# Latent attention layers: 96 query columns a head in three tiles instead of 128 in four, with the rotary swap moved to the keys

## The chip, the cores and the metric

One NeuronCore of a Trainium2 chip runs the whole program: a first block (a sparse and a gated linear mixer with a feed-forward part) and a second block of four attention layers on 512 tokens of width 1024, all in float32. The metric is the device time of one execution in microseconds.

## What is computed

Only layers 0 and 3 of the second block are touched. They are latent attention layers: queries come from a 384-wide latent `cq` through `w_q_up`, which gives each of 16 heads 96 columns, 64 plain and 32 that are rotated with the token's position.

```python
q = (_rmsnorm(cq, q_norm) @ w_q_up).reshape(B, S, MLA_HEADS, MLA_NOPE_DIM + MLA_ROPE_DIM)
q_rope = _apply_rope(q[..., MLA_NOPE_DIM:], cos[:, None, :], sin[:, None, :])
k_rope = _apply_rope(k_rope, cos, sin)
q_full = jnp.concatenate([q[..., :MLA_NOPE_DIM], q_rope], axis=-1)
scale = (MLA_NOPE_DIM + MLA_ROPE_DIM) ** -0.5
o = _dense_causal(q_full, k_full, v, scale).reshape(B, S, MLA_WIDTH)
# _apply_rope: x1, x2 are the halves of the 32 columns
jnp.concatenate([x1 * cos - x2 * sin, x2 * cos + x1 * sin], axis=-1)
```

## The kernel before

Every product is done three times (`mm3`, lines 269 to 277): each float32 operand is split by `split_into` into a high part (ScalarE, line 214) and a low part (VectorE, line 215), and the products high by high, low by high and high by low are added up in PSUM. Features stand on the partitions, the 512 tokens along the free dimension.

A latent layer works through four quads of four heads, and in each quad through two pairs (`pr`). Per quad it loads and splits `qw` (query weights), `kvw` (key and value weights) and the weights of two gate tiles, multiplies the values `vt`, and then, per pair, the keys of both heads into `k4h`, `k4l` and, per head, the queries. For the queries the weights are laid out with 128 columns: 64 plain, 32 rotary, and the same 32 again with halves swapped. So one product of 3 x 3 matmuls gives a `pj` tile of 128 rows, 64 of them x and swapped x. VectorE multiplies these 64 rows by a table of cosines and sines in place (line 1083), and `split_gain` makes `qh` (ScalarE, line 218) and `ql` (VectorE, line 219). The scores add the two rotary halves up by themselves, because the keys hold the same 32 rotated rows twice. `dense_head` then runs the softmax of the head block by block (scores `s` by line 273 ff., masked maximum line 324, exponent line 327, division line 331, transposes line 337), and `dense_values` multiplies by the values into `o` (line 350).

Instructions are ordered by the framework's scheduler at build time. Each engine runs its own list strictly in that order, so an instruction that waits holds up everything behind it. PSUM has three `pj` tiles, two `s`, two `t` and one `o`. `og` (8 tiles of 512 columns) holds the gated outputs of the layer, `vt` has two buffers, and the raw weight tile `wr` has three.

Of the kernel before, what the change touches and what calls it, by code (L numbers as in the profile page):

```python
# [18 lines left out]
S = 512  # L19
D = 1024  # L20
NB = 4
# [31 lines left out]
def shape_constants():  # L53
# [33 lines left out]
    sc = np.float32(96 ** -0.5)  # L87
    tab = np.empty((128, S), np.float32)
    for base in (0, 64):
        tab[base:base + 16] = tab[base + 16:base + 32] = cos.T * sc  # L90
        tab[base + 32:base + 48], tab[base + 48:base + 64] = -sin.T * sc, sin.T * sc
    out["mla_tab"] = tab
    kr = np.concatenate([cos, cos, -sin, sin], axis=1)
# [34 lines left out]
class Net:  # L128
# [857 lines left out]
    def mla(self, i, j, last):  # L986
        nc, a, tc = self.nc, self.a, self.tc
        w = a["mla_w_in_2"][j]
        with ExitStack() as c1:
            l1 = c1.enter_context(tc.tile_pool(name="l1", bufs=1))  # L990

            tab = self.load_const(l1, "mla_tab")
            scale = l1.tile([128, 2], F32, name="scale")
# [6 lines left out]
            with tc.tile_pool(name="pre", bufs=1) as pre:  # L1000
# [9 lines left out]
                for b in range(NB):  # L1010
                    ps = self.pj()
                    self.proj_tok(ps[:, 0:288], wk, self.act, b, cols=slice(0, 288))
                    self.low_rank(pre, cn[:, b, 384:640], ps, 256)
                    t = pre.tile([128, 64], F32, name="krt", bufs=2)
                    nc.vector.tensor_tensor(out=t[:, 0:32], in0=ps[:, 256:288], in1=kro[:, b, 0:32], op=ALU.mult)
                    nc.vector.tensor_tensor(out=t[:, 32:48], in0=ps[:, 272:288], in1=kro[:, b, 32:48], op=ALU.mult)
                    nc.vector.tensor_tensor(out=t[:, 48:64], in0=ps[:, 256:272], in1=kro[:, b, 48:64], op=ALU.mult)
                    for r0 in (0, 32, 64, 96):
                        nc.vector.tensor_tensor(out=kr[:, b, r0:r0 + 32], in0=t[:, 0:32], in1=t[:, 32:64], op=ALU.add)
                for c in range(6):  # L1020
# [17 lines left out]
            for quad in range(4):  # L1038

                qw = []  # L1040
                for pr in range(2):
                    v = self.wload(wqu, 0, 3, (quad * 384 + pr * 192, 192))
                    h, l = self.wtile(3, 256)
                    for u in range(2):
                        r, s0 = 64 - 64 * u, u * 96
                        pieces = ((0, 0, 96),) if u == 0 else ((192, 0, 64), (128, 64, 32))
                        for d, c, n in pieces + ((128 * u + r + 32, 80, 16), (128 * u + r + 48, 64, 16)):
                            self.split_into(h[:, :, d:d + n], l[:, :, d:d + n], v[:, :, s0 + c:s0 + c + n])
                    qw.append(Split([(0, 3, h, l)]))
# [21 lines left out]
                for pr in range(2):  # L1071
# [3 lines left out]
                    for hh in range(2):  # L1075
                        r = slice(64 * hh, 64 * hh + 64)
                        self.split_into(keys[hh][0][r], keys[hh][1][r], ps[r])
                    pt = []
                    for hh in range(2):
                        ps = self.pj()  # L1080
                        self.proj_feat(ps, qw[pr], cq, kc=3, cols=slice(hh * 128, hh * 128 + 128))
                        r = slice(64 - 64 * hh, 128 - 64 * hh)
                        nc.vector.tensor_tensor(out=ps[r], in0=ps[r], in1=tab[r], op=ALU.mult)
                        q = [l2.tile([128, S], F32R, name=n) for n in ("qh", "ql")]
                        self.split_gain(*q, ps, scale[:, hh:hh + 1])

                        def scores(ps, m, n):
                            (ah, al), (bh, bl) = ((t[:, m] for t in q), (t[:, n] for t in keys[hh]))
                            self.mm3(ps, [((ah, al), (bh, bl))])

                        pt.append(self.dense_head(P, scores))
# [253 lines left out]
```

## Time and profile before

| What | Value |
|---|---|
| time, median of 3 runs | 1871.92 us (1871.9 to 1871.92) |
| profiled execution | 1871.62 us, its span 1869.8 us |
| TensorE matmul busy (PE) | 1827.8 us, 98% of the span |
| VectorE busy (DVE) | 1149.3 us, 61% |
| ScalarE busy (ACT) | 873.6 us, 47% |
| granted TensorE clock | 0.999 of full speed |

The span runs from the first to the last instruction of the profiled execution; 1.8 us lie outside of it. A busy share is a mean over the whole span. Matmuls are pipelined, so the recorded length of one is longer than the distance to the next: the distance of the starts is what a matmul costs.

### The profile page before, as it was taken

To read this page: it belongs to the slowest core of one execution; us is meant where nothing else is said; L and a number is where in the kernel's file an instruction comes from. 1 tells how busy PE (TensorE), PEld (TensorE's weight loads), DVE (VectorE), ACT (ScalarE), POOL (GpSimd) and SP (SyncE) were. 2 spreads that over 40 slices of the span, in tenths; PEclk is the share of its full clock that TensorE was granted. 3 is DMA by queue.
4 is the path that set the end of the run, shared out by engine and by line. 5 is a ranking of instruction groups with operands and counts; after the bars stand their busy time and mean duration, and the time that the engine had idled before them with its cause. 6 is when DMAs were issued, how large, how long until landed. Compare 5 with 4: busy or idle time off the path is not lost.

```text
span 1869.8 us, 26625 instructions
## 1 busy us (share of the span) xinstructions
PE 1827.8 (98%) x9843; PEld 1489.1 (80%) x9843; DVE 1149.3 (61%) x2954; ACT 873.6 (47%) x1970; POOL 156.1 (8%) x213
## 2 busy tenths in 40 slices
PE   7999999999999999999999999999999999999997
PEld 6877787678888888889887788877888877988775
DVE  5564487854533244346878675576776666787866
ACT  4543336743322132235667434463566564366651
POOL 2211200000000000002000011241000000200001
PEclk9999999999999999999999999999999999999999
DMA  7222141042432253224221133221432322232111
GB/s 218 80 57 57 37 126 40 29 135 79 125 91 84 66 143 90 73 67 122 59 69 57 48 103 91 72 63 38 114 79 54 82 70 79 75 87 59 46 57 45
DMA packets 200781, 148.09 MB, mean 79 GB/s; under 512 B 8797, under 2 KB 178570, under 8 KB 200650
## 3 DMA queue, kind: packets, MB, share of 16 engines
q1 hardware_dynamic: 198858, 140.97, 26.2%
q0 software_dynamic: 1792, 5.42, 0.9%
q8 instruction: 77, 1.26, 0.3%
q14 instruction: 54, 0.44, 0.1%
HBM read 144.27 MB, written 2.10 MB: 78 GB/s over the span
## 4 chain that ended last, share of the span: by engine, by line
PE 91%; DVE 3%; ACT 2%; issue 2%; DMA 1%; POOL 0%; SPq 0%; POOLq 0%; DVEq 0%; ACTq 0%
PE pj L273 25%; PE pj L275 24%; PE pj L276 24%; PE o L350 4%; PE t L337 3%; PE s L311 1%; PE s L275 1%; PE s L273 1%; PE s L276 1%; PE t L372 1%; PE s L614 1%; PE s L312 1%; DVE wl L215 1%; ACT pt L205 1%; PE t L1198 1%
## 5 line engine op out<-in xcount | busy, mean ns | idle before, releaser
L214 ACT ACTIVATE wh<-wr 128x1024 fp32r<-128x1024 f32 (+9 forms) x390 | 280.4, 749 | 467.1 <-PE pj L275 279.8
L215 DVE TENSOR_TENSOR wl<-wr,wh 128x1024 fp32r<-128x1024 f32 (+9 forms) x390 | 321.7, 847 | 229.1 <-ACT wh L214 224.7
L273 PE MATMUL pj<-Ah,wh 128*128 128x512 f32 (+1 forms) x1120 | 435.4, 389 | 1.3 <-DVE k4l L215 0.8
L275 PE MATMUL pj<-Al,wh 128*128 128x512 f32 (+1 forms) x1120 | 434.1, 388 | 0.0
L276 PE MATMUL pj<-Ah,wl 128*128 128x512 f32 (+1 forms) x1120 | 433.5, 388 | 0.0
L273 PEld LDWEIGHTS pj<-Ah,wh 128*128 128x128 f32 x1120 | 210.8, 188 | 45.7 <-PE s L276 1.6
L276 PEld LDWEIGHTS pj<-Ah,wl 128*128 128x128 f32 x1120 | 210.8, 188 | 44.2 <-issue 1.5
L275 PEld LDWEIGHTS pj<-Al,wh 128*128 128x128 f32 x1120 | 210.8, 188 | 42.6 <-issue 0.8
L273 PE MATMUL pj<-wh,Ah 128*128 128x512 f32 (+5 forms) x640 | 217.6, 341 | 4.7 <-ACT Ah L214 4.6
L275 PE MATMUL pj<-wl,Ah 128*128 128x512 f32 (+5 forms) x640 | 215.7, 337 | 0.0
L276 PE MATMUL pj<-wh,Al 128*128 128x512 f32 (+5 forms) x640 | 213.3, 338 | 2.0 <-DVE Al L215 1.9
L327 ACT ACTIVATE sp<-sp,nm 128x128 f32<-128x128 f32 (+3 forms) x256 | 142.9, 559 | 75.5 <-DVE nm L326 73.4
L205 ACT ACTIVATE pt<-t 128x512 f32<-128x512 f32 (+3 forms) x288 | 115.2, 445 | 106.0 <-PE t L337 66.5
L324 DVE CUSTOM_DVE_ANT_0 sp<-s,c_causal 128x128 f32<-128x128 f32 (+3 forms) x256 | 121.0, 486 | 56.6 <-PE s L276 23.5
L273 PEld LDWEIGHTS pj<-wh,Ah 128*128 128x128 f32 x640 | 120.5, 188 | 19.5 <-ACT Ah L214 7.3
L276 PEld LDWEIGHTS pj<-wh,Al 128*128 128x128 f32 x640 | 120.2, 188 | 13.9 <-DVE Al L215 3.0
L275 PEld LDWEIGHTS pj<-wl,Ah 128*128 128x128 f32 x640 | 120.5, 188 | 10.8 <-issue 0.2
L337 PE MATMUL t<-ident,sp 128*128 128x128 f32 x640 | 109.0, 278 | 5.1 <-ACT pt L205 4.8
L337 PEld LDWEIGHTS t<-ident,sp 128*128 128x128 f32 x640 | 77.3, 140 | 30.8 <-ACT pt L205 12.7
L331 DVE TENSOR_SCALAR sp<-sp,rc 128x128 f32<-128x128 f32 (+3 forms) x256 | 96.7, 383 | 5.0
L276 PE MATMUL pj<-wh,hdl 128*128 128x512 f32 x176 | 68.3, 389 | 0.0
L275 PE MATMUL pj<-wl,hdh 128*128 128x512 f32 x176 | 68.3, 390 | 0.0
(417 smaller groups left out, 2822.5 us busy)
## 6 DMA issues: line engine op xcount, KB each, us to landing
wr<-in_w_in_dram SPq DMA_DIRECT2D x34, 512.0 KB, 3.9
wr<-in_fox_w_in_dram SPq DMA_DIRECT2D x30, 512.0 KB, 4.1
wr<-in_w_ffn_gate_dram SPq DMA_DIRECT2D x22, 512.0 KB, 3.8
wr<-in_w_ffn_up_dram SPq DMA_DIRECT2D x22, 512.0 KB, 3.8
wr<-in_w_ffn_down_dram SPq DMA_DIRECT2D x20, 512.0 KB, 3.7
wr<-in_swa_w_in_dram SPq DMA_DIRECT2D x20, 512.0 KB, 4.8
wr<-in_mla_w_in_dram SPq DMA_DIRECT2D x16, 512.0 KB, 4.3
wr<-in_mla_w_out_dram SPq DMA_DIRECT2D x16, 512.0 KB, 3.8
```

The costliest lines, as they stand in the source:

```text
L205: return self.nc.scalar.activation(out, in_, AF.Copy, scale=1.0 if scale is None else scale)
L214: self.nc.scalar.activation(h, src, AF.Copy)
L215: self.nc.vector.tensor_tensor(out=l, in0=src, in1=h.bitcast(F32), op=ALU.subtract)
L273: mm = self.nc.tensor.matmul(ps, lhsT=ah, rhs=bh, start=i == 0, stop=False)
L275: self.nc.tensor.matmul(ps, lhsT=ah, rhs=bl, start=False, stop=False)
L276: mm = self.nc.tensor.matmul(ps, lhsT=al, rhs=bh, start=False, stop=i == n - 1)
L311: self.nc.tensor.matmul(ps, lhsT=q, rhs=kh, start=True, stop=False)
L324: nc.vector.tensor_tensor_reduce(out=v, in0=ps, in1=self.causal[:, S - n:S], scale=1.0, scalar=LOWEST, op0=ALU.add, op1=ALU.max, accum_out ...
L327: nc.scalar.activation(v, v, AF.Exp, bias=nm[:, g], accum_out=sm[:, g])
L331: nc.vector.tensor_scalar(v, v, rc[:, g], None, ALU.mult)
L337: nc.tensor.transpose(ps[:, (b - j) * 128:(b - j + 1) * 128], sp[:, POFF[b] + j * 128:POFF[b] + j * 128 + 128], self.ident)
L350: mm = self.nc.tensor.matmul(po[64 * i:64 * i + 64, j * 128:S], lhsT=value(j, i), rhs=pt[:, TOFF[j]:TOFF[j] + (NB - j) * 128], start=first ...
```

## The change

The weights of a quad are laid out as three tiles of 128 columns with nothing twice: two tiles (`qw[0]`, 256 columns) each hold one head of the first pair whole and the rotary columns of one head of the second pair; one tile (`qw[1]`) holds the plain columns of both heads of the second pair. They are gathered by seven loads instead of two, and split by two operations an engine instead of fourteen. The swap of the halves goes to the keys, whose second copy is made from swapped products. In the first pair, each head's tile is multiplied on 32 rows at a time by a cosine and a sine table: twice in place for its own queries, twice out into `qf` for a head of the second pair. In the second pair, the plain rows are copied into `qf` by ScalarE and `qf` is split from SBUF. `qf` lies in the last two tiles of `og` in quads 0 to 2 and in a `vt` buffer in quad 3.

```diff
@@ mla, tables
-            tab = self.load_const(l1, "mla_tab")
+            cos, sin = self.load_const(l1, "mla_cos"), self.load_const(l1, "mla_sin")
@@ mla, rotary keys, per block of 128 tokens
-                    for r0 in (0, 32, 64, 96):
-                        nc.vector.tensor_tensor(out=kr[:, b, r0:r0 + 32], in0=t[:, 0:32], in1=t[:, 32:64], op=ALU.add)
+                    kv = kr[:, b].rearrange("p (u c) -> p u c", u=2)
+                    tv = lambda o, n: t[:, None, o:o + n].to_broadcast([128, 2, n])
+                    nc.vector.tensor_tensor(out=kv[:, :, 0:32], in0=tv(0, 32), in1=tv(32, 32), op=ALU.add)
+                    nc.vector.tensor_tensor(out=kv[:, :, 32:48], in0=tv(16, 16), in1=tv(48, 16), op=ALU.add)
+                    nc.vector.scalar_tensor_tensor(out=kv[:, :, 48:64], in0=tv(0, 16), scalar=-1.0, in1=tv(32, 16), op0=ALU.mult, op1=ALU.subtract)
@@ mla, query weights of a quad
-                qw = []
-                for pr in range(2):
-                    v = self.wload(wqu, 0, 3, (quad * 384 + pr * 192, 192))
-                    h, l = self.wtile(3, 256)
-                    for u in range(2):
-                        r, s0 = 64 - 64 * u, u * 96
-                        pieces = ((0, 0, 96),) if u == 0 else ((192, 0, 64), (128, 64, 32))
-                        for d, c, n in pieces + ((128 * u + r + 32, 80, 16), (128 * u + r + 48, 64, 16)):
-                            self.split_into(h[:, :, d:d + n], l[:, :, d:d + n], v[:, :, s0 + c:s0 + c + n])
+                o, qw = quad * 384, []
+                for ranges in (((0, 96), (256, 32), (160, 32), (352, 32), (96, 64)), ((192, 64), (288, 64))):
+                    v = self.wload(wqu, 0, 3, *((o + c, n) for c, n in ranges))
+                    h, l = self.wtile(3, v.shape[-1])
+                    self.split_into(h, l, v)
                     qw.append(Split([(0, 3, h, l)]))
@@ mla, queries of a pair
+                    if pr == 0:
+                        room = og[:, KD - 2:KD] if quad < 3 else l2.tile([128, NB, 256], F32, name="vt").rearrange("p (h c) n -> p h (c n)", h=2)
+                        qf = [room[:, hh] for hh in range(2)]
+                    else:
+                        ps = self.pj()
+                        self.proj_feat(ps, qw[1], cq, kc=3)
+                        for hh in range(2):
+                            r = slice(64 * hh, 64 * hh + 64)
+                            self.acopy(qf[hh][r], ps[r], 96 ** -0.5)
                     for hh in range(2):
-                        ps = self.pj()
-                        self.proj_feat(ps, qw[pr], cq, kc=3, cols=slice(hh * 128, hh * 128 + 128))
-                        r = slice(64 - 64 * hh, 128 - 64 * hh)
-                        nc.vector.tensor_tensor(out=ps[r], in0=ps[r], in1=tab[r], op=ALU.mult)
                         q = [l2.tile([128, S], F32R, name=n) for n in ("qh", "ql")]
-                        self.split_gain(*q, ps, scale[:, hh:hh + 1])
+                        if pr == 0:
+                            ps = self.pj()
+                            self.proj_feat(ps, qw[0], cq, kc=3, cols=slice(hh * 128, hh * 128 + 128))
+                            own, other = (slice(64 - 64 * hh + c, 96 - 64 * hh + c) for c in (0, 32))
+                            for out, src, tab in ((qf[hh][own], other, cos), (qf[hh][other], other, sin), (ps[other], own, sin), (ps[own], own, cos)):
+                                nc.vector.tensor_tensor(out=out, in0=ps[src], in1=tab[src], op=ALU.mult)
+                            self.split_gain(*q, ps, scale[:, hh:hh + 1])
+                        else:
+                            self.split_into(*q, qf[hh])
```

The scheduler makes new lists for both layers. Lines of the changed kernel in these layers are named by their own numbers (215 and 219 are 211 and 215 there, 324 is 320, and 1093 is the multiplication by the tables).

VectorE at the first two heads of quad 0, before: `pj_7319` is the keys' product, `pj_7330` and `pj_7405` are the queries' products of heads 0 and 1, `k4l` the keys' low part, `wl_7712` a split of gate weights of the next quad.

```order
L215 TENSOR_TENSOR k4l_6771<-pj_7319,k4h_6770 64x512
L215 TENSOR_TENSOR k4l_6771<-t_7152,k4h_6770 64x512
L1083 TENSOR_TENSOR pj_7330<-pj_7330,c_mla_tab_6761 64x512
L215 TENSOR_TENSOR k4l_6771<-pj_7319,k4h_6770 64x512
L219 SCALAR_TENSOR_TENSOR ql_7342<-pj_7330,scale_6763,qh_7341 128x512
L1083 TENSOR_TENSOR pj_7405<-pj_7405,c_mla_tab_6761 64x512
L215 TENSOR_TENSOR wl_7712<-wr_7709,wh_7711 128x1024
L219 SCALAR_TENSOR_TENSOR ql_7417<-pj_7405,scale_6763,qh_7416 128x512
```

The same place in the changed kernel: `pj_7311` and `pj_7389` are the queries' products of heads 0 and 1, `pj_7475` the keys' product of the second pair, `wl_7668` and `wl_7674` the two splits of gate weights.

```order
L1093 TENSOR_TENSOR og_6769<-pj_7311,c_mla_cos_6761 32x512
L1093 TENSOR_TENSOR og_6769<-pj_7311,c_mla_sin_6763 32x512
L211 TENSOR_TENSOR k4l_6773<-pj_7298,k4h_6772 64x512
L1093 TENSOR_TENSOR pj_7311<-pj_7311,c_mla_sin_6763 32x512
L1093 TENSOR_TENSOR og_6769<-pj_7389,c_mla_cos_6761 32x512
L1093 TENSOR_TENSOR og_6769<-pj_7389,c_mla_sin_6763 32x512
L1093 TENSOR_TENSOR pj_7311<-pj_7311,c_mla_cos_6761 32x512
L211 TENSOR_TENSOR wl_7668<-wr_7665,wh_7667 128x1024
L1093 TENSOR_TENSOR pj_7389<-pj_7389,c_mla_sin_6763 32x512
L211 TENSOR_TENSOR wl_7674<-wr_7671,wh_7673 128x1024
L211 TENSOR_TENSOR k4l_6773<-pj_7475,k4h_6772 64x512
L215 SCALAR_TENSOR_TENSOR ql_7310<-pj_7311,scale_6765,qh_7309 128x512
```

From head 0's product to its `ql` stood two other operations of VectorE, the table's product and a key split; now eleven stand there, both gate splits among them.

VectorE at the first two heads of quad 3, before: `pj_8731` and `pj_8806` are the queries' products of the two heads. The values' products of quad 2's two pairs are taken over (line 982) 25 and 58 operations behind the last of these rows.

```order
L215 TENSOR_TENSOR k4l_6771<-pj_8720,k4h_6770 64x512
L1083 TENSOR_TENSOR pj_8731<-pj_8731,c_mla_tab_6761 64x512
L215 TENSOR_TENSOR k4l_6771<-pj_8720,k4h_6770 64x512
L324 ISA sp_8494,mx_8495<-s_8517,c_causal_360 128x384
L324 ISA mx_8495 128x1
L326 TENSOR_SCALAR nm_8496<-mx_8495 128x1
L324 ISA sp_8494,mx_8495<-s_8526,c_causal_360 128x512
L324 ISA mx_8495 128x1
L219 SCALAR_TENSOR_TENSOR ql_8743<-pj_8731,scale_6763,qh_8742 128x512
L1083 TENSOR_TENSOR pj_8806<-pj_8806,c_mla_tab_6761 64x512
```

The same place in the changed kernel: `o_8558` is the values' product of quad 2's second pair, `vt_8641` the `vt` buffer that holds `qf` in quad 3, `pj_8644` and `pj_8722` are the queries' products of the two heads, and `s_8665` the first scores of quad 3.

```order
L978 SCALAR_TENSOR_TENSOR og_6769<-o_8558,og_6769 128x512
L1093 TENSOR_TENSOR vt_8641<-pj_8644,c_mla_cos_6761 32x512
L1093 TENSOR_TENSOR vt_8641<-pj_8644,c_mla_sin_6763 32x512
L1093 TENSOR_TENSOR vt_8641<-pj_8722,c_mla_cos_6761 32x512
L1093 TENSOR_TENSOR vt_8641<-pj_8722,c_mla_sin_6763 32x512
L1093 TENSOR_TENSOR pj_8644<-pj_8644,c_mla_sin_6763 32x512
L1093 TENSOR_TENSOR pj_8722<-pj_8722,c_mla_sin_6763 32x512
L1093 TENSOR_TENSOR pj_8644<-pj_8644,c_mla_cos_6761 32x512
L1093 TENSOR_TENSOR pj_8722<-pj_8722,c_mla_cos_6761 32x512
L215 SCALAR_TENSOR_TENSOR ql_8643<-pj_8644,scale_6765,qh_8642 128x512
L215 SCALAR_TENSOR_TENSOR ql_8721<-pj_8722,scale_6765,qh_8720 128x512
L320 ISA sp_8660,mx_8661<-s_8665,c_causal_360 128x128
```

The rotation of quad 3's queries stood ahead of the end of quad 2; now it stands behind it, because its buffer is the one from which quad 2's values are read.

## Rows read from the trace of the kernel before

**Rows 1.** The page: the span, and busy time, share and instructions of each engine.

```profile
span 1869.8 us, 26625 instructions
PE 1827.8 (98%) x9843; PEld 1489.1 (80%) x9843; DVE 1149.3 (61%) x2954; ACT 873.6 (47%) x1970; POOL 156.1 (8%) x213
```

**Rows 2.** The page: the chain that ended last, by engine.

```profile
PE 91%; DVE 3%; ACT 2%; issue 2%; DMA 1%; POOL 0%; SPq 0%; POOLq 0%; DVEq 0%; ACTq 0%
```

**Rows 3.** Who PE waited for, 866 to 1095 us: us, times, longest; first, last of seven.

```profile
PE pj L273 <- ACT Ah L214: 0.9, 2, 0.7
...
PE s L273 <- DVE mx L324: 0.2, 1, 0.2
```

**Rows 4.** Busy time by stretch: quad 0's, quad 1's, quad 2's start (PE, PEld, DVE, ACT).

```profile
890.00:905.00 15.00, 14.62 (x70) 11.85 (x69) 12.97 (x27) 10.18 (x24) 0.00 (x0) 1.00 0.18 56
926.00:948.00 22.00, 22.00 (x117) 17.38 (x116) 19.76 (x63) 14.93 (x40) 0.00 (x0) 1.00 0.23 62
968.00:986.00 18.00, 17.78 (x100) 13.95 (x99) 15.16 (x47) 12.33 (x29) 0.00 (x0) 1.00 0.18 59
```

**Rows 5.** Timeline of PE, quad 0: start, length, line, tiles.

```profile
893.94 0.39 PE L273 MATMUL pj<-cth,wh 128*128 128x512 f32 x1
...
896.04 0.40 PE L273 MATMUL pj<-cth,wh 128*128 128x512 f32 x1
...
897.44 0.22 PE L273 MATMUL s<-k4h,qh 128*128 128x128 f32 x1
...
904.08 0.47 PE L273 MATMUL pj<-Ah,wh 128*128 128x512 f32 x1 [0.38 <-DVE k4l L215]
```

**Rows 6.** Timeline of DVE, quad 0.

```profile
894.14 0.71 DVE L1083 TENSOR_TENSOR pj<-pj,c_mla_tab 64x512 f32<-64x512 f32 x1 [0.20 <-PE pj L276]
894.88 0.69 DVE L215 TENSOR_TENSOR k4l<-pj,k4h 64x512 fp32r<-64x512 f32 x1
895.61 0.75 DVE L219 SCALAR_TENSOR_TENSOR ql<-pj,scale,qh 128x512 fp32r<-128x512 f32 x1
```

**Rows 7.** Timeline of DVE, quad 1: the table's product of two neighbouring heads.

```profile
939.14 0.71 DVE L1083 TENSOR_TENSOR pj<-pj,c_mla_tab 64x512 f32<-64x512 f32 x1
939.88 0.16 DVE L328 RECIPROCAL rc<-sum 128x1 f32<-128x1 f32 x1
...
942.12 0.69 DVE L1083 TENSOR_TENSOR pj<-pj,c_mla_tab 64x512 f32<-64x512 f32 x1
942.73 0.44 DVE L215 TENSOR_TENSOR wl<-wr,wh 128x288 fp32r<-128x288 f32 x1
```

**Rows 8.** Groups of DVE by shape, both layers: busy, mean ns; idle before.

```profile
L215 DVE TENSOR_TENSOR wl<-wr,wh 128x1024 fp32r<-128x1024 f32 x206 | 252.3, 1226 | 191.5 <-ACT wh L214 189.4 <-PE pj L276 0.5
L1083 DVE TENSOR_TENSOR pj<-pj,c_mla_tab 64x512 f32<-64x512 f32 x32 | 22.4, 700 | 4.4 <-PE pj L276 3.7
L215 DVE TENSOR_TENSOR wl<-wr,wh 128x48 fp32r<-128x48 f32 x64 | 10.4, 199 | 0.0
L215 DVE TENSOR_TENSOR wl<-wr,wh 128x288 fp32r<-128x288 f32 x16 | 7.3, 453 | 6.1 <-ACT wh L214 5.9
L215 DVE TENSOR_TENSOR q<-sp,q 16x512 fp32r<-16x512 f32 x1 | 0.7, 680 | 0.0
```

**Rows 9.** Groups of ACT by shape, both layers.

```profile
L218 ACT ACTIVATE qh<-pj,scale 128x512 fp32r<-128x512 f32 x32 | 22.1, 690 | 14.0 <-PE s L275 7.5 <-DVE pj L1083 6.1
L214 ACT ACTIVATE k4h<-pj 64x512 fp32r<-64x512 f32 x32 | 18.8, 587 | 6.2 <-DVE k4l L215 3.5 <-PE pj L276 2.3
```

**Rows 10.** Timeline of PE, first layer: end of quad 2's second pair, and layer's end.

```profile
1025.58 2.37 PE L350 MATMUL o<-pt,vt 128*64 128x512 f32 x16
1027.89 0.33 PE L337 MATMUL t<-ident,sp 128*128 128x128 f32 x1
...
1061.10 0.71 PE L337 MATMUL t<-ident,sp 128*128 128x128 f32 x3 [0.58 <-ACT pt L205]
```

**Rows 11.** The page's DMA issues: the query weights (KB each, us to landing).

```profile
wr<-in_mla_w_q_up_dram SPq DMA_DIRECT2D x16, 288.0 KB, 3.0
```

More of the change, by code (lines that the diff above doesn't have):

```diff
@@ L87, in shape_constants @@
     sc = np.float32(96 ** -0.5)
[L88 to L92, printed above, removed]
+    out["mla_cos"], out["mla_sin"] = np.tile(cos.T * sc, (8, 1)), np.tile(sin.T * sc, (8, 1))
     kr = np.concatenate([cos, cos, -sin, sin], axis=1)
```

## Prediction

> **What bounds the kernel now.** I read the page first. TensorE is busy for 98% of the span and makes up 91% of the chain that ended last [rows 1, 2]. So time is saved only where TensorE has less to do, and lost wherever it has to wait. Next I asked whom it waits for in the first latent layer: seven kinds of waits, 9 in number, together 3.8 us of 229 [rows 3]. So in these layers nothing is left to win but work, and nearly every new wait is a loss. Then the busy times by stretch, at the start of a quad, where keys and queries are made: VectorE works 13.0 of 15 us, 19.8 of 22 and 15.2 of 18 [rows 4]. TensorE is ahead by little there: VectorE, at 61% over the span, is at 83 to 90% just where this change gives it more. Last the order of quad 0: head 0's query product ends when VectorE starts on it at 894.14, its `ql` is done at 896.36, and its first scores start at 897.44 [rows 5, 6]. That is 1.1 us of slack.
>
> **What is taken away.** A product of 3 x 3 matmuls takes 896.04 - 893.94 = 2.10 us from start to start [rows 5], 0.233 us a matmul. A quad has three such products for queries instead of four; over four quads and two layers 72 matmuls go, 72 x 0.233 = 16.8 us. TensorE is the bound, so all of that would be gained if nothing waited. Its matmuls keep their shapes, so no other price enters here.
>
> **What VectorE and ScalarE get.** The multiplication by the tables is on 32 rows, and no row of before has 32 rows by 512. From both sides: 64x512 takes 0.70 us and 16x512 takes 0.68 [rows 8], so 32 rows take 0.69, and half the rows save nothing. Four operations a quad become eight.
>
> What lies between two of them? Where the rows of head 0 (64 to 127) were multiplied, the next operation started at 939.88, 0.03 us after the end; where those of head 1 (0 to 63) were, the next started at 942.73, 0.08 us ahead of the end [rows 7]. I take the longer, 0.73 us from start to start, since the new operations start on rows 0, 32, 64 and 96 in turn; 0.62 is the other bound. The Trainium skill has a rule for this (VectorE: DVE Perf Modes, Two Vector instructions with no wait between them): an operation whose tensors start in another group of 32 partitions than the last ones is held until all earlier ones have finished. The trace agrees in both rows; by the rule nearly all eight are held, 5.8 us a quad, and without it 5.0.
>
> So VectorE gets 4 x 0.73 = 2.9 us a quad. It gives back weight splits: fourteen pieces (eight of 48 columns at 0.20 us, two of 288 at 0.45, four between) become one of 768 and one of 384. Between the rows of 288 and 1024 columns these would cost 0.96 and 0.55 [rows 8]; that is about 3.7 less 1.5, so 2.2 us back. Net some 0.7 us a quad on an engine with 39% idle: as an average it is nothing. ScalarE wins splits likewise and gets two copies of 64x512 at 0.59 [rows 9]. The rotary keys go from four additions a block to three operations, ahead of the quads and under gate products: nothing, and some tenths if that cover went.
>
> **What the order makes of it.** The price is in the places where TensorE arrives before the queries.
>
> Quad 0: TensorE's list up to the first scores is the same as before, so head 0's product is again done at 894.14 and TensorE is at the scores at 897.5. VectorE's list then has seven operations up to the last one on head 0's tile: 7 x 0.73 = 5.1, to 899.25. `qh` takes 0.69 more [rows 9]: 900.0, and TensorE has waited 2.5 us. It does four short score matmuls (0.45 us) and needs `ql`. On VectorE, two gate splits (1.2 each), one table operation, one key split and `ql` itself stand ahead: 4.6 us from 899.25, 903.85. TensorE waits another 3.4. Together 5.9; a wait of before just behind it, 0.4 [rows 5], is then covered: 5.5. Behind the waiting scores stand the second pair's query product and the gates of quad 1, which are held up with them. At 0.62 between the operations it would be 4.5.
>
> Quads 1 and 2: TensorE has 10 us of other work between head 0's product and its scores, so the queries are in time; but VectorE is handed 8 instead of 2 table operations in one run, 4.4 us, and loses two of the second pair's (1.4) in the same stretch. That is 3.0 us more where 2.2 and 2.8 were idle [rows 4], and while it lags, `pj` and `s` tiles come free late. From 0 (the idle time takes it) to 3.0 (none of it does); I take half, 1.5 each.
>
> Quad 3: `qf` now lies in the `vt` buffer of quad 2, so the rotation stands behind the values' product of quad 2's second pair. Two of three `pj` tiles stay taken by unrotated queries until then; the third waits for ScalarE's two copies into the same buffer, 2 x 0.59 = 1.2 us, with TensorE idle. Ahead of that product, quad 2's last softmax was covered by quad 3's scores and gates; TensorE had no gap around its values' product (1025.58 + 2.31 = 1027.89) [rows 10]. Now only one product of 2.1 us is left as cover. An uncovered turn from transposition to ScalarE's copy cost 0.58 us at the layer's end [rows 10]; four such turns make 2.3. Together 3.5, with bounds of 1.2 (copies alone) and 5.4 (the softmax of the last block uncovered too).
>
> The layer's end: quad 3's heads 2 and 3 come later, with fewer fillers; from 0 to two more turns (1.2), I take 0.5.
>
> The sum: 5.5 + 1.5 + 1.5 + 3.5 + 0.5 = 12.5 us a layer, 25.0 in both; less 16.8 it is 8.2 us slower. The profiled execution took 1871.62, its span and 1.8 around it, and the median is 1871.92, so they stand for each other: 1871.9 + 8.2 = 1880. The bounds: with all upper ends 5.5 + 3 + 3 + 5.4 + 1.2 = 18.1 a layer, 1891; with all lower ends 4.5 + 1.2 = 5.7 a layer, 1866.5.
>
> **Rivals.** *VectorE catches up* (faster). While TensorE waits in quad 0, VectorE works its list off, and the later quads run as far apart as before. For it speaks VectorE's idle time in the rest of the layer; against it that its list at quads 1 to 3 repeats quad 0's. Then only quad 0 (5.5) and the copies (1.2) count: 13.4 - 16.8 = -3.4, and with quad 0 at half, too, -8.9: 1863 to 1868.5. It decides at 8.4 us of waits a layer: below that the change is faster.
>
> *Even.* The waits come to between 6.6 and 10.2 us a layer, and 16.8 is eaten up: 1872. For it: my middle terms are halves of ranges.
>
> *The loads come late* (slower still). A quad's query weights come in seven loads instead of two; a load of 288 KB landed in 3.0 us, and the loads stand in one queue [rows 11]. If each quad's weights came 2 us late on ScalarE, whose list would stop, it would be up to 16 us on top: 1896. Against it: the loads are issued a quad ahead. The Trainium skill (DMA: Bandwidth & Descriptors, Specifications) wants at least 512 bytes in one piece for full rate; the new pieces have 128, 256 and 384 bytes and the old had 768. No row of before shows what that costs here.
>
> That the 72 matmuls do not go is no rival: the built lists have 312 of these where there were 384.
>
> **How the numbers follow.** Forecast, waits above the gain: 0.52. VectorE catches up: 0.25. Even: 0.17. Late loads: 0.06. A change of 0.2%, 3.7 us, is about what a measurement of this kernel can tell from none. Faster 0.25, same 0.17, slower 0.58. The range takes in most of the faster rival and the upper bounds: 1862 to 1892; within the forecast alone 1876 to 1891.
>
> **What would show it.** In the changed profile: 72 fewer query matmuls; 32x512 table operations of 0.69 us, 0.73 apart in a run; a gap of TensorE of 2 to 3 us ahead of quad 0's first scores and one of 3 ahead of their low part, in both layers; a gap of over 1 us behind quad 2's last values' product, ended by ScalarE's copy. It is wrong if these gaps are under half of that, if the 32-row operations are shorter than 0.6, or if gaps show up at query weights that DMA ends.

## The result, and the profile after

The changed kernel takes 1896.21 us, median of four runs (1893.91 to 1897.47), beside 1871.91 for the kernel before on the same chip: 1.0125 of it, 95% interval 1.0113 to 1.0137, so 24.3 us slower. The prediction was 1880, 8.1 slower, with a range to 1892. The direction was right, the size three times too small.

The profiled execution took 1897.47. Its page, the lines that answer to [rows 1] and [rows 2]:

```profile
span 1895.7 us, 26431 instructions
...
PE 1828.9 (96%) x9771; PEld 1484.3 (78%) x9771; DVE 1157.4 (61%) x2882; ACT 871.7 (46%) x1890; POOL 155.2 (8%) x213
...
PE 88%; DVE 6%; ACT 3%; issue 2%; DMA 1%; POOL 0%; SPq 0%; POOLq 0%; DVEq 0%; ACTq 0%
```

72 matmuls are gone (9843 to 9771), yet TensorE's share fell from 98% to 96%, and VectorE went from 3% to 6% of the chain that ended last. VectorE is busy for nearly the same time as before (1157.4 us, 1149.3 before): over the whole execution its sum of work hardly changed.

Where is the time? A latent layer is measured here from the matmul out of `cth` (the normed latents, high part) that waits for ScalarE, to the first matmul of its output product, which waits for ScalarE's `Ah`. TensorE's timeline of the kernel before, first latent layer:

```profile
887.63 0.39 PE L273 MATMUL pj<-wh,cth 128*128 128x256 f32 x1 [0.67 <-ACT cth L218]
...
1065.29 0.50 PE L273 MATMUL pj<-wh,Ah 128*128 128x512 f32 x1 [0.73 <-ACT Ah L214]
```

and of the changed kernel:

```profile
887.67 0.39 PE L269 MATMUL pj<-wh,cth 128*128 128x256 f32 x1 [0.67 <-ACT cth L214]
...
1076.50 0.50 PE L269 MATMUL pj<-wh,Ah 128*128 128x512 f32 x1 [0.74 <-ACT Ah L210]
```

177.7 us became 188.8. The second layer went from 178.2 (1653.01 to 1831.18) to 192.4 (1664.58 to 1856.99), read in the same way. That is 11.2 and 14.2 us, 25.4 together, of the 25.9 by which the span grew. As 8.4 us of matmuls went from each, the layers wait 19.6 and 22.6 us more than before; forecast were 12.5 each.

Who TensorE waited for from 866 to 1106 us (in total, times, longest; first four of thirteen lines), to be held against the seven kinds and 3.8 us of [rows 3]:

```profile
PE t L333 <- ACT pt L201: 4.8, 6, 1.6
PE s L272 <- DVE ql L215: 2.6, 1, 2.6
PE s L269 <- ACT qh L214: 2.1, 1, 2.1
PE pj L269 <- ACT vt L201: 1.3, 1, 1.3
```

The thirteen lines sum to 16.1 us, 12.3 more than before. The other 7.3 us of the 19.6 stand in no list of waits; the table below finds them in lower clock and in gaps that are longer than the idle time named in them.

Quad 0. TensorE's timeline, answering to [rows 5]:

```profile
897.69 0.39 PE L272 MATMUL pj<-cth,wl 128*128 128x512 f32 x1
900.18 0.33 PE L269 MATMUL s<-k4h,qh 128*128 128x128 f32 x1 [2.10 <-ACT qh L214]
...
900.62 0.41 PE L271 MATMUL s<-k4l,qh 128*128 128x256 f32 x1
903.59 0.79 PE L272 MATMUL s<-k4h,ql 128*128 128x128 f32 x2 [2.55 <-DVE ql L215]
904.18 0.63 PE L269 MATMUL pj<-cth,wh 128*128 128x512 f32 x1
904.61 0.63 PE L271 MATMUL pj<-ctl,wh 128*128 128x512 f32 x1
```

VectorE's, answering to [rows 6]:

```profile
894.16 0.70 DVE L1093 TENSOR_TENSOR og<-pj,c_mla_cos 32x512 f32<-32x512 f32 x1 [0.19 <-PE pj L272]
...
896.33 0.71 DVE L1093 TENSOR_TENSOR pj<-pj,c_mla_sin 32x512 f32<-32x512 f32 x1
897.06 0.68 DVE L1093 TENSOR_TENSOR og<-pj,c_mla_cos 32x512 f32<-32x512 f32 x1
...
898.48 0.70 DVE L1093 TENSOR_TENSOR pj<-pj,c_mla_cos 32x512 f32<-32x512 f32 x1
899.21 1.22 DVE L211 TENSOR_TENSOR wl<-wr,wh 128x1024 fp32r<-128x1024 f32 x1
...
902.81 0.73 DVE L215 SCALAR_TENSOR_TENSOR ql<-pj,scale,qh 128x512 fp32r<-128x512 f32 x1
```

The first table operation starts at 894.16, the seventh in VectorE's list at 898.48, and it ends at 899.18; the forecast had 899.25. TensorE is at the scores at 897.92 (the last product's 0.23 after 897.69) and starts them at 900.18. The low part waits for `ql` until 903.59; the forecast had 903.85. The last two rows to be read are 904.18 and 904.61: matmuls of 512 columns are now 0.63 us long and start 0.43 apart, where before the waits they were 0.39 long and 0.23 apart, and from 907.53 on they are so again. That is TensorE's lower clock.

The busy times by stretch, answering to the first two lines of [rows 4] (granted clock in the third column from the end):

```profile
890.00:905.00 15.00, 10.13 (x44) 7.65 (x43) 13.16 (x18) 7.24 (x12) 0.00 (x0) 0.85 0.21 51
926.00:948.00 22.00, 21.38 (x117) 16.69 (x116) 21.16 (x61) 16.18 (x39) 0.00 (x0) 1.00 0.22 52
```

In quad 0's stretch TensorE works 10.1 us instead of 14.6, at a clock of 0.85. In quad 1's VectorE works 21.16 of 22.

To size the terms I took TensorE's timeline row by row: a gap is the time from one start to the next less the usual pitch of that shape (0.233 us at 512 columns), summed where it is over a quarter of a microsecond, and before's gaps in the same quad are taken off. Matmuls at the lower clock are kept apart, by their lengths (slow products of the values are not; they stand in quad 3). A gap is longer than the idle time in its row: 2.26 against 2.10 and 2.85 against 2.55 in quad 0. Us more than before:

| place | forecast | first layer | second layer |
|---|---|---|---|
| quad 0 | 5.5 | 5.4 | 5.4 |
| quad 1 | 1.5 | 1.2 | 1.9 |
| quad 2 | 1.5 | 4.5 | 3.4 |
| quad 3 | 3.5 | 4.5 | 7.8 |
| layer's end | 0.5 | 1.5 | 0.6 |
| lower clock | none | 2.8 | 3.5 |
| sum | 12.5 | 19.9 | 22.6 |

The sums agree with the 19.6 and 22.6 from the layers' lengths to 0.3 us. A single row is good to about 0.5 us, since it depends on the pitches taken.

### The profile page after: what moved, and what is told of

It reads as the page before. It is cut to its first block, busy times and chain, and to the rows that moved or that the text cites. A ratio compares the mean times of both kernels' runs of the same rounds, so it can differ in the third digit from the quotient of the medians.

```text
span 1895.7 us, 26431 instructions
## 1 busy us (share of the span) xinstructions
PE 1828.9 (96%) x9771; PEld 1484.3 (78%) x9771; DVE 1157.4 (61%) x2882; ACT 871.7 (46%) x1890; POOL 155.2 (8%) x213
## 4 chain that ended last, share of the span: by engine, by line
PE 88%; DVE 6%; ACT 3%; issue 2%; DMA 1%; POOL 0%; SPq 0%; POOLq 0%; DVEq 0%; ACTq 0%
PE pj L269 24%; PE pj L271 23%; PE pj L272 23%; PE o L346 4%; PE t L333 3%; ACT pt L201 1%; DVE wl L211 1%; DVE sp L320 1%; PE s L307 1%; PE s L272 1%; PE s L269 1%; PE t L368 1%; PE s L271 1%; PE s L610 1%; PE s L308 1%
## 5 line engine op out<-in xcount | busy, mean ns | idle before, releaser
L210 ACT ACTIVATE wh<-wr 128x1024 fp32r<-128x1024 f32 (+6 forms) x294 | 269.0, 923 | 476.8 <-PE pj L271 300.1
L211 DVE TENSOR_TENSOR wl<-wr,wh 128x1024 fp32r<-128x1024 f32 (+6 forms) x294 | 310.7, 1064 | 227.3 <-ACT wh L210 223.1
L272 PEld LDWEIGHTS pj<-wh,Al 128*128 128x128 f32 x640 | 120.7, 189 | 12.6 <-DVE Al L211 1.7
L333 PE MATMUL t<-ident,sp 128*128 128x128 f32 x640 | 112.6, 280 | 13.3 <-ACT pt L201 13.0
L333 PEld LDWEIGHTS t<-ident,sp 128*128 128x128 f32 x640 | 77.8, 140 | 42.2 <-ACT pt L201 24.0
L327 DVE TENSOR_SCALAR sp<-sp,rc 128x128 f32<-128x128 f32 (+3 forms) x256 | 96.3, 383 | 4.6
```

The lines of the kernel that those rows point to most:

```text
L210: self.nc.scalar.activation(h, src, AF.Copy)
L211: self.nc.vector.tensor_tensor(out=l, in0=src, in1=h.bitcast(F32), op=ALU.subtract)
L272: mm = self.nc.tensor.matmul(ps, lhsT=al, rhs=bh, start=False, stop=i == n - 1)
L327: nc.vector.tensor_scalar(v, v, rc[:, g], None, ALU.mult)
L333: nc.tensor.transpose(ps[:, (b - j) * 128:(b - j + 1) * 128], sp[:, POFF[b] + j * 128:POFF[b] + j * 128 + 128], self.ident)
```

## The experiments

Two theories were held against each other, and two rivals beside them; the first two do not exclude each other. *Queue*: TensorE waits because VectorE has eight table operations in one run ahead of the first head, and because quad 3 writes into quad 2's `vt` buffer. *Work*: VectorE simply has too much to do, wherever it stands. *Loads*: the seven narrow loads come late. *Gain*: the 72 matmuls were never worth 16.8 us. Ratios are to the kernel before, run beside each; "layers" is the change of both latent layers' lengths against before, from the profiled run (the changed kernel: 1.0125, layers +25.4).

| run | ratio, 95% interval | layers, us |
|---|---|---|
| e1_own_qf | 1.0052, 1.0037 to 1.0067 | +8.9 |
| e2_two_ops | 0.9990, 0.9981 to 0.9999 | -2.7 |
| e3_three_products | 0.9917, 0.9901 to 0.9934 | -14.5 |
| e4_two_loads | 1.0141, 1.0125 to 1.0156 | +26.0 |
| e5_before_eight | 1.0039, 1.0024 to 1.0054 | +9.1 |
| e6_two_ops_quad0 | 1.0054, 1.0039 to 1.0069 | +12.6 |
| e7_late_half | 1.0118, 1.0101 to 1.0135 | +20.6 |
| e8_late_half_own | 1.0002, 0.9992 to 1.0011 | +1.0 |
| e9_late_half_pool | 0.9964, 0.9952 to 0.9977 | -7.7 |
| e10_two_ops_own | 0.9941, 0.9926 to 0.9956 | -11.4 |
| e11_filler | 1.0103, 1.0089 to 1.0117 | +21.9 |
| e12_two_ops_quads12 | 1.0074, 1.0060 to 1.0088 | +12.5 |

**e1: another buffer in quad 3.**

```
-room = og[:, KD - 2:KD] if quad < 3 else l2.tile([128, NB, 256], F32, name="vt")...
+room = og[:, KD - 2:KD] if quad < 3 else self.wraw.tile([128, 1024], F32, name="wr")...
```

> The changed kernel, with one edit: in quad 3 the half-finished queries `qf` get a weight-load buffer (`wr`) of their own instead of the `vt` buffer of quad 2. In the changed kernel TensorE's waits around quad 3 (from quad 2's last softmax to the layer's last scores) grew by 4.1 us in the first latent layer and 6.7 in the second, and 1.3 us of lower clock come with them in the second. If the buffer is the cause, most of that goes: 8 to 12 us less than the changed kernel, 1884 to 1888, and the gap behind quad 2's last values' product that ScalarE's copy ends is gone. If the rotation itself is the cause (its eight operations stand in VectorE's way wherever they write), at most 3 us go: 1893 to 1896.

Measured: 16.6 us less than the changed kernel in the layers, 13.7 by the ratios, more than was expected either way. TensorE's timeline of this run at the place where the changed kernel waited for ScalarE's copies:

```profile
1020.50 0.50 PE L269 MATMUL pj<-Ah,wh 128*128 128x512 f32 x1 [0.78 <-ACT wr L201]
```

The copies are still waited for, 0.78 us, but they no longer stand behind quad 2's values' product. The shared `vt` buffer costs more than the waits around quad 3: without it the rest of the layer's order changes too (quad 2's gaps fall from 5.8 to 3.0 us in the first layer).

**e2: half the table operations.** Rows stay where they are, so the rotation is not computed.

```
-for out, src, tab in ((qf[hh][own], other, cos), (qf[hh][other], other, sin), (ps[other], own, sin), (ps[own], own, cos)):
+for out, tab in ((qf[hh][both], cos), (ps[both], sin)):   # both: the head's 64 rows; in0 is ps[both]
```

> The changed kernel, with two table operations of 64 rows a head instead of four of 32; the rotary part of the queries is then not that of the reference (no rows change places), all else stays. VectorE's run of eight operations at a quad's start becomes four, 2.9 us less. If TensorE waits for this run, the first gap of quad 0 (2.1 us, ended by ScalarE's `qh`) goes to nothing, the second (2.55, ended by `ql`) shrinks by about the same, the lower clock behind them goes too (1.6 us a layer), and the waits of quads 2 and 3 shrink by 1 to 2 us each: 12 to 18 us less than the changed kernel, 1878 to 1884. If the loads or the missing gain of the matmuls are the cause, it stays at 1896 within 3 us.

Measured: 28.1 us less in the layers, 25.3 by the ratios, well over the 12 to 18 that were expected. Quad 0 has no gap left, and in the first layer quad 2's two gaps come to 1.1 us; quad 3 alone still has its 7.2. So the sixteen operations a layer that went were worth more than their own 0.73 us each (23 us in both layers).

**e3: the matmuls alone.**

```
+if pr * hh == 0:
     ps = self.pj()
     self.proj_feat(ps, qw[pr], cq, kc=3, cols=slice(hh * 128, hh * 128 + 128))
```

> The kernel before, without the query product of each quad's fourth head, which reads the third head's product again (its queries are not those of the reference); VectorE, ScalarE and the loads do the same work as before. This prices the 72 matmuls alone. If they are worth their 0.233 us each: 1855 (16.8 us less). If TensorE without them only waits longer for VectorE, which is nearly as late, less than half is left: 1864 to 1870.

Measured: 14.5 us less in the layers, and 0.0083 of 1872, 15.5 us, by the ratio. The gain was real: nearly all of the 16.8 us is there when nothing else changes. *Gain* falls.

**e4: two loads instead of seven.**

```
-for ranges in (((0, 96), (256, 32), (160, 32), (352, 32), (96, 64)), ((192, 64), (288, 64))):
+for ranges in (((0, 256),), ((256, 128),)):
```

> The changed kernel, with the query weights of a quad in two loads of neighbouring columns (256 and 128) instead of seven of 32 to 96 columns; the columns then stand in another order, so the queries are not those of the reference. If late or slow loads are a part of the cause, it is faster by 5 us or more, 1891 or less. If not, it stays within 2 us: 1894 to 1898.

Nothing came back: the median is 1899.25, even 1.3 us above what was expected without an effect. The page's line on DMA packets, of the changed kernel and then of this run:

```profile
DMA packets 217067, 148.60 MB, mean 78 GB/s; under 512 B 30973, under 2 KB 194602, under 8 KB 216938
```

```profile
DMA packets 201068, 148.60 MB, mean 78 GB/s; under 512 B 8830, under 2 KB 178603, under 8 KB 200939
```

22,143 small packets fewer, and the same time. *Loads* falls, although its price in the prediction, 1896, is the time that was measured. The Trainium skill (DMA: Bandwidth & Descriptors, Specifications) wants 512 bytes in one piece for full rate; here nobody waited for that rate, and no wait of TensorE in the changed kernel's thirteen lines is ended by a DMA.

**e5: eight operations in the kernel before.**

```
-nc.vector.tensor_tensor(out=ps[r], in0=ps[r], in1=tab[r], op=ALU.mult)
+for r in (slice(64 - 64 * hh, 96 - 64 * hh), slice(96 - 64 * hh, 128 - 64 * hh)):
+    nc.vector.tensor_tensor(out=ps[r], in0=ps[r], in1=tab[r], op=ALU.mult)
```

> The kernel before, with each of the four table operations of a quad (64 rows) cut into two of 32 rows: eight 32-row operations a quad as in the changed kernel, but two for each head, in front of that head's own scores, and all four products kept. VectorE gets 2.9 us more a quad. If that work alone makes TensorE wait, wherever it stands, most of the 26 us that the two 64-row operations gave back show up here: 1885 to 1897. If it is that all eight stand in front of the first head's scores, it stays near the kernel before: 1872 to 1877.

Measured: 1.0039, 9.1 us in the layers, between the two expectations. TensorE's timeline, quad 0:

```profile
898.44 0.33 PE L273 MATMUL s<-k4h,qh 128*128 128x128 f32 x1 [0.23 <-ACT qh L218]
...
900.46 0.50 PE L276 MATMUL s<-k4h,ql 128*128 128x128 f32 x2 [1.29 <-DVE ql L219]
```

With two operations ahead of each head the first scores wait 0.23 us instead of 2.10 and the low part 1.29 instead of 2.55. So in the kernel before, where each head's two operations stand ahead of that head alone, the added work costs 9.1 us, a third of the 28.1 that halving the operations gave back in the changed kernel (e2). That the other two thirds are the place of the operations follows only as far as the two kernels can be compared; e7 to e9 give *Work* more.

**e6 and e12: quads one by one.** Two operations a head as in e2, in quad 0 alone, or in quads 1 and 2 alone.

```
+for out, src, tab in steps[quad == 0]:          # e6
+for out, src, tab in steps[quad in (1, 2)]:     # e12
```

> The changed kernel, with two table operations of 64 rows a head in quad 0 alone (its queries are not those of the reference), four of 32 in quads 1 to 3. The prediction put 5.5 us of waits a layer on quad 0; the changed kernel's trace shows 5.5 and 1.6 to 2.0 of lower clock behind them, 14 us in both layers. If these are quad 0's own, 12 to 15 us less than the changed kernel: 1881 to 1884. If the time only moves on to the later quads (VectorE's backlog), 3 to 7 us less: 1889 to 1893.

> The changed kernel, with two table operations of 64 rows a head in quads 1 and 2 (their queries are not those of the reference), four of 32 in quads 0 and 3. The prediction gave these two quads 1.5 us of waits a layer each, 6.0 in both layers. The changed kernel's trace has gaps there that are 11 us longer than before in both layers, with about 1.5 us of lower clock. If the gaps are the rotation's: 10 to 13 us less than the changed kernel, 0.9934 to 0.9947 of it. If the prediction's half of VectorE's lag was right, and the rest of the gaps are only quad 3's and quad 0's waits handed on: 5 to 7 us less, 0.996 to 0.9974.

Measured: 12.8 us less in the layers for quad 0 (13.3 by the ratios), as was expected of its own waits, and 12.9 for quads 1 and 2 (9.5 by the ratios, just under what was expected of the whole run). In the layers they add: 25.7 of e2's 28.1. So in the main each quad pays its own waits. Not wholly: in e12 quad 3's gaps in the first layer rose from 4.8 to 7.5 us, with another order of the list there. In e6 TensorE works 14.58 of 15 us from 890 to 905 at a clock of 1.00, where the changed kernel had 10.13 and 0.85.

**e7 and e8: half of the rotation later.** ScalarE copies the rows of heads 2 and 3 out unrotated; VectorE multiplies them behind head 1's `ql`. e8 has e1's buffer as well.

```
+self.acopy(qf[hh][other], ps[other])                     # heads 0 and 1
-for out, src, tab in (... four ...):
+for out, tab in ((ps[other], sin), (ps[own], cos)):
+for out, tab in ((qf[hh][own], cos), (qf[hh][other], sin)):   # heads 2 and 3
+    op = nc.vector.tensor_tensor(out=out, in0=qf[hh][other], in1=tab[other], op=ALU.mult)
+    self.after(op.ins, low)
```

> The changed kernel with the rotation of heads 2 and 3 put off: ScalarE copies their 32 unrotated rows out of the two PSUM tiles (about 0.6 us each), and their four table operations run on VectorE behind the low part `ql` of head 1, out of SBUF. The reference's result. VectorE's run ahead of the first scores falls from eight operations to four, and ScalarE gets eight more copies a layer. If the run ahead of the first head is the cause, 10 to 20 us less than the changed kernel: 1876 to 1886 (quad 3's buffer is still that of `vt`). If VectorE's sum of work is, at most 4: 1892 to 1897.

> The kernel with the rotation of heads 2 and 3 put off, and a weight-load buffer for quad 3's `qf` as in the first experiment: both causes taken away together, the reference's result. If they add, 14 us less than with the rotation put off alone and 20 to 34 less than the changed kernel: 1862 to 1874, with the 16.8 us of the matmuls as the floor, 1855. If the two overlap (quad 3's wait is the run of eight again), it is within 4 us of the rotation put off alone.

e7 came out at 1895.72, within what was expected if VectorE's sum of work is the cause: 4.8 us less in the layers, and by the ratio no clear difference from the changed kernel. But two things go against each other in it. Quad 0's two gaps fell from 5.1 to 1.75 us, but in quad 3 four copies of ScalarE instead of two now stand behind the values' product. TensorE's timeline of e7 there:

```profile
1024.44 4.07 PE L346 MATMUL o<-pt,vt 128*64 128x512 f32 x16 [0.37 <-ACT pt L201]
1031.03 0.50 PE L269 MATMUL pj<-Ah,wh 128*128 128x512 f32 x1 [2.52 <-ACT vt L201]
```

The wait is 2.52 where it was 1.29, and the product ahead of it ran at the lower clock (4.07 us; 2.38 in the changed kernel). With the buffer, e8, it is 19.6 less than e7, 24.4 less than the changed kernel, as was expected if the two causes add, and level with before: the gain of the matmuls is just eaten up. The fair comparison is with e1, which has the same buffer: there, putting half of the rotation off is worth 7.9 us of the layers (8.9 to 1.0), while two operations fewer a head are worth 20.3 (8.9 to -11.4, e10). So putting work later did not bring back all that fewer operations bring; e8 also pays for eight more copies of ScalarE a layer, which no run separates. In the first layer's middle quads VectorE's `mx` ends most of the waits that are left (2.9 of 3.3 us).

**e9: that half on GpSimd.** As e8, with `nc.gpsimd.tensor_tensor` for the put-off operations and no order imposed.

> The kernel of the last run (rotation of heads 2 and 3 put off, own buffer in quad 3), with the four put-off table operations of a quad on GpSimd, which stands idle in these layers, instead of VectorE; the reference's result. VectorE then has four table operations a quad, as many as before the change. If VectorE's backlog is what ate the 16.8 us (its `mx` and `ql` end most of the waits left in that run's middle quads), this is faster than the kernel before by 5 to 13 us: 0.993 to 0.997 of it. If GpSimd is so slow that the second pair's queries come late, or its work slows VectorE down, it is level with before or slower: 1.000 to 1.006.

0.9964, as was expected if VectorE's backlog ate the gain: this kernel, which leaves nothing out, is faster than both, by 6.7 us than the one before. GpSimd's timeline, quad 0:

```profile
896.51 1.28 POOL L1099 TENSOR_TENSOR og<-og,c_mla_cos 32x512 f32<-32x512 f32 x1 [20.00 <-ACT og L201]
...
899.41 1.98 POOL L1099 TENSOR_TENSOR og<-og,c_mla_cos 32x512 f32<-32x512 f32 x1 [0.23 <-ACT og L201]
```

An operation takes 1.28 to 1.98 us there, and 0.685 on VectorE in e8 (shown at the end), but GpSimd does not appear among those whom TensorE waits for. The Trainium skill (GPSIMD Engine Reference, Engine selection) advises VectorE for elementwise work, as GpSimd is about twice as slow with two inputs; the rows show a factor of 1.9 to 2.9, and the time does not follow it: what was gained is time in VectorE's list. From e8 to e9 the layers win 8.7 us; e9 changes two things, the engine and the order imposed in e8, and no run separates them.

**e10: both causes gone.** e1 and e2 together.

> The changed kernel with both named causes taken away: two table operations of 64 rows a head (the queries are then not those of the reference) and an own buffer for quad 3's `qf`. If these two are all that stands against the 16.8 us, it comes to where the kernel before comes with its matmuls taken away (0.992 of before): 0.990 to 0.994. If there is a third cause (loads, keys, ScalarE's copies), it stays above 0.996.

0.9941, 11.4 us less than before in the layers: most of e3's 14.5, and at the edge of what was expected without a third cause. Of the 42.2 us of waits in the changed kernel (25.4 and the 16.8 of the matmuls), the 28.1 of e2 and 8.7 of buffer (e2 to e10) leave 5.4 open. The buffer's 8.7 here are 16.6 in e1: what the two edits give back overlaps by 7.9 us. TensorE's gaps are 5.2 longer than before's, among them waits of 0.64 and 1.50 at quad 3 that ScalarE's copies of `qf` end, which no edit took away.

**e11: spare work in the waits.**

```
+if quad == 0 and hh == 1:
+    for spare in range(2):
+        self.proj_feat(self.pj(), qw[0], cq, kc=3, cols=slice(0, 128))
```

> The changed kernel with more work for TensorE: in quad 0 the first head's query product is made twice more into spare PSUM tiles that nobody reads, 18 matmuls a layer, 4.2 us, and in its list most of them stand where TensorE waits for the rotation. If TensorE's lower clock behind quad 0 (1.6 us lost in the first latent layer, 2.0 in the second, by the lengths of its matmuls) comes of its standing still there, the clock stays up, the spare work costs nothing and 2 to 4 us are won: 0.998 to 0.999 of the changed kernel. If the clock falls whatever it does, the spare work still fits into the waits: no difference within 1 us. If it does not fit, up to 8 us slower.

18 matmuls more a layer, and the layers are 3.5 us shorter; the whole run is 0.998 of the changed kernel, though the two intervals overlap a little. The stretch from 895 to 910 us by busy time, in the changed kernel and in this run:

```profile
895.00:910.00 15.00, 10.13 (x37) 7.50 (x36) 13.07 (x25) 7.46 (x13) 0.00 (x0) 0.77 0.18 49
```

```profile
895.00:910.00 15.00, 14.73 (x67) 11.56 (x66) 13.82 (x27) 7.37 (x13) 0.00 (x0) 1.00 0.22 59
```

The clock stays at 1.00 (2.4 GHz) where it fell, and TensorE does 67 matmuls instead of 37. So the lower clock of quad 0 comes of standing still. That fits the Trainium skill (TensorE: Matmul & The Clock Gate, What's actually happening), by which the clock follows how busy the engine has been.

## Why the prediction was right in its signs and wrong in its size

The forecast was 12.5 us of waits a layer, and 19.6 and 22.6 came. The steps that failed are the term for quad 2, over its upper bound in both layers, the term for quad 3, over it in the second layer, and the lower clock, which the sum had at nothing.

**What held.** 72 matmuls went, worth 15 of the 16.8 us (e3). A 32x512 operation takes 0.69 to 0.70 us, and four in a row start 0.73, 0.70, 0.72 and 0.73 apart (896.33 to 899.21, the third at 897.76); 0.73 was right and 0.62 was not. The Trainium skill's rule on two Vector instructions with no wait between them (VectorE: DVE Perf Modes) fits: each starts only after the end of the one ahead. Quad 0 came out as worked out, to 0.3 us in each time. That the sum agrees, 5.4 against 5.5, is in part luck: the two gaps are 2.26 and 2.85 for 2.5 and 3.4, and one of 0.38 at 896.44, which the forecast did not have, makes up for it. Quad 1 came to 1.2 and 1.9 against 1.5; the tile that comes free late is there (TensorE waits for `ql` of VectorE at 942.37), but the half was a guess. ScalarE's two copies in quad 3 took 1.29 against 1.2, and there the first layer's four turns (0.46, 0.87, 0.64, 0.37) took the 2.3 that was put down. The gap behind quad 2's last values' product is where it was foretold:

```profile
1025.85 2.38 PE L346 MATMUL o<-pt,vt 128*64 128x512 f32 x16 [0.37 <-ACT pt L201]
1029.52 0.50 PE L269 MATMUL pj<-Ah,wh 128*128 128x512 f32 x1 [1.29 <-ACT vt L201]
```

**What failed: quad 2, "I take half".** It cost 4.5 and 3.4 us, over the upper bound of 3.0, and e12 shows that it is the rotation of quads 1 and 2 itself. The step counted VectorE's lag against VectorE's idle time over the stretch. What TensorE waits for is one operation, and that comes when all ahead of it in its engine's list is done. Its timeline at the largest gap of quad 2, second layer:

```profile
1756.17 0.28 PE L272 MATMUL s<-k4h,ql 128*128 128x256 f32 x1
1758.76 0.50 PE L269 MATMUL pj<-cth,wh 128*128 128x512 f32 x1 [2.31 <-DVE ql L215]
```

The `ql` of the first head (1757.95 to 1758.70) stands in VectorE's list behind its own head's four table operations, the first two of the other head, a weight split and some of the softmax, which run with hardly a pause from 1750.32 on. Before, a head had one table operation. At the same place of the first layer another engine is the one waited for:

```profile
978.04 0.28 PE L272 MATMUL s<-k4h,ql 128*128 128x256 f32 x1
979.96 0.44 PE L333 MATMUL t<-ident,sp 128*128 128x128 f32 x2 [1.64 <-ACT pt L201]
```

ScalarE's timeline just ahead of it:

```profile
976.70 0.69 ACT L214 ACTIVATE qh<-pj,scale 128x512 fp32r<-128x512 f32 x1
...
978.12 1.04 ACT L210 ACTIVATE wh<-wr 128x1024 fp32r<-128x1024 f32 x1
979.06 0.58 ACT L210 ACTIVATE k4h<-pj 64x512 fp32r<-64x512 f32 x1
979.54 0.53 ACT L201 ACTIVATE pt<-t 128x256 f32<-128x256 f32 x2
```

TensorE waits for ScalarE's `pt` copy of the last head, and that copy stands in ScalarE's list behind `qh`, an exponent of the softmax, a weight split and a key part, which run with hardly a pause. `qh` starts at 976.70, when VectorE has just ended its fourth operation on that tile (976.66); but a weight split ahead of it in ScalarE's own list ends then too, so the rows do not show that the rotation held it. That a late operation on VectorE holds up a third engine's list is likely here, not shown. Another 1.16 us of this layer's quad 2 end with ScalarE's copies of `qf` (TensorE waits 0.99 for `og` at 989.34), which the forecast priced in quad 3 alone.

**What failed: quad 3, 3.5.** In the first layer 4.5, within its bounds. In the second it cost 7.8, over the bound of 5.4: there the turns of quad 2's last softmax were longer, and the clock fell. TensorE's timeline, second layer:

```profile
1795.47 0.61 PE L333 MATMUL t<-ident,sp 128*128 128x128 f32 x3
1797.85 0.93 PE L333 MATMUL t<-ident,sp 128*128 128x128 f32 x5 [1.77 <-ACT pt L201]
...
1799.01 0.63 PE L271 MATMUL pj<-ctl,wh 128*128 128x512 f32 x1
1799.43 0.63 PE L272 MATMUL pj<-cth,wl 128*128 128x512 f32 x1
...
1803.67 0.71 PE L333 MATMUL t<-ident,sp 128*128 128x128 f32 x3 [1.18 <-ACT pt L201]
1804.75 4.07 PE L346 MATMUL o<-pt,vt 128*64 128x512 f32 x16 [0.37 <-ACT pt L201]
1810.11 0.50 PE L269 MATMUL pj<-Ah,wh 128*128 128x512 f32 x1 [1.29 <-ACT vt L201]
```

1.77, 1.18, 0.37 and 1.29 us of waits, matmuls 0.42 to 0.43 apart behind the first of them, and the values' product 4.07 us instead of 2.38. The identical layer does not pay an identical price, as its list is another; I took one layer's terms twice.

**What was missing: the lower clock.** The prediction counted the time in which TensorE stands, and nothing for what comes after. It is 2.8 and 3.5 us, a third of what was missing, and e11 shows for quad 0 that it belongs to the standing.

Of the 17.2 us that the waits came out larger than forecast (42.2 instead of 25.0), quad 2 has 4.9, quad 3 5.3 (1.7 of it the slow values' product), the lower clock elsewhere 6.3, and the other places about 1.

**The rivals.** *VectorE catches up* fell: quads 1 to 3 have waits that go with their own edits (e12, e1). *Even* fell with it. *The loads come late* had the right time by a mechanism that isn't there (e4). What e9 shows is nearer to the first: with four table operations a quad on VectorE, as many as before, the change is a gain. What stays open is how the cost of the rotation divides between VectorE's sum of work and the place of the operations: e5 and quad 0's gaps in e7 speak for the place, e8 beside e10 for the work.

## What to carry to other kernels

When work moves onto an engine that has time to spare on average, ask what will stand behind it in that engine's list and in the list of the next engine, and price it there; an idle share over a stretch does not say that the operation waited for comes in time. Put a price on what follows a wait, too: the 5.4 us that TensorE stood in quad 0 brought 1.6 to 2.0 us more in lower clock. An idle slow engine can be a good place for work that nobody waits for.

## What the runs showed of the hardware

In quad 0 of the first layer TensorE stood for 2.26 us, did four short matmuls and stood for 2.85 us. Its granted clock by stretch (third column from the end):

```profile
897.50:900.50 3.00, 0.90 (x6) 0.46 (x4) 2.89 (x5) 2.22 (x3) 0.00 (x0) 1.00 0.00 0
900.70:903.50 2.80, 0.34 (x2) 0.04 (x1) 2.80 (x4) 0.59 (x1) 0.00 (x0) 0.50 0.38 76
```

It was at its lower level (1.2 of 2.4 GHz) just behind the first wait, so the second, longer one is not what brought it down; the matmuls from 904.18 to 907.5 ran at that level. In e5 it fell behind waits of 0.23 and 1.29 us (0.50 from 901.6 to 904.9). In quad 3 of the second layer a values' product of 16 matmuls took 4.07 us at it, 2.38 at the upper one in the first layer.

GpSimd's work is not free for VectorE where the two meet. In e8, where VectorE does it all, the groups of VectorE by shape, 888 to 1062 us (busy, mean ns):

```profile
L327 DVE TENSOR_SCALAR sp<-sp,rc 128x512 f32<-128x512 f32 x16 | 7.7, 484 | 0.2
...
L1099 DVE TENSOR_TENSOR og<-og,c_mla_sin 32x512 f32<-32x512 f32 x6 | 4.1, 685 | 0.2
```

In e9 the mean of the 16 operations of L327 is 540 ns. One of them makes the difference; GpSimd's and VectorE's timelines:

```profile
975.23 1.35 POOL L1099 TENSOR_TENSOR og<-og,c_mla_sin 32x512 f32<-32x512 f32 x1
975.47 1.39 DVE L327 TENSOR_SCALAR sp<-sp,rc 128x512 f32<-128x512 f32 x1
```

It overlaps an operation of GpSimd, takes 1.39 us, and ends 0.28 us behind it; the other 15 overlap none and take 0.47 to 0.49. In the second layer the one that meets GpSimd takes 1.30.

What lies ahead of the first latent layer is the same work in all kernels, and still that layer began at 887.6 to 891.6 us after the start in their traces; so changes of a few microseconds are better read from a layer's own length than from the whole time.
